# Second block of a two-block layer: attention output in its own tiles, no sums on GpSimd, a denser interleave of the state space branch

## The chip, the cores and the metric

The kernel runs on one core of one Trainium2 chip. The metric is the device time of one execution in microseconds (us); lower is better. The five engines are written as the profile writes them: PE (TensorE, with PEld for its weight loads), DVE (VectorE), ACT (ScalarE), POOL (GpSimd) and SP (SyncE, which here issues the DMAs).

## The reference, cut to what matters

A sequence of 1024 tokens of width 1024 passes two blocks. The first (attention, a gated delta rule, sixteen experts) is not touched. The second is, in outline:

```python
h = rms(x, norm1_g);  proj = h @ w_in
u, q, k, v, qi, ki, wi, gates = split(proj)
y_ssm = s5_branch(u, ...)              # complex state space scan, 32 groups of 64 states, gelu, GLU
# sparse attention, 8 blocks of 128 queries, 8 heads of 64, one shared key/value head
iscore = sum_h relu(qi_h . ki) * wi_h   # index scores, causal
idx = top_k(iscore, 256)                # 256 keys kept per query
y_att = softmax(q k[idx]^T / 8) v[idx]
g_ssm, g_att = split(gates)
merged = sigmoid(g_ssm) * (y_ssm @ w_proj_ssm) + sigmoid(g_att) * (y_att @ w_proj_attn)
x = x + merged @ w_out
x = x + (silu(h2 @ w_ffn_gate) * (h2 @ w_ffn_up)) @ w_ffn_down      # h2 = rms(x, norm2_g)
```

## The kernel before, in words

Products in float32 precision are made of three matmuls: each operand is split into a high and a low part (`split`: ACT rounds, a subtraction gives the rest), and `mm3` adds high*high, high*low and low*high in PSUM. Weights come the same way: `wunit` loads a raw tile, ACT makes `wh`, and `K.sub` (L76) makes `wl`. `K.sub` is VectorE's subtraction, except in the middle of `stage_attn`, where it is set to GpSimd's.

`stage_norm2` normalises the input in eight tiles of 128 tokens and leaves it transposed in `K.hh` and `K.hl`; in every second tile the product with the final gain (L1645) is GpSimd's. `idx_tile` and `q_tile` make index scores, keys, values and queries. `select` finds the 256 largest scores of each query by a search over 32 bits, two blocks at a time: one block's counts are ACT's (L1775), the other's DVE's (L1778), and a few one-column operations on DVE (L1781 to L1793) lead from one bit to the next. `attend` then computes one block of 128 queries in four steps (a generator, one `yield` a step): scores in the PSUM tile `lg`, a masked maximum on DVE (L1875), the exponential on ACT (L1878), a scaling (POOL for blocks 0 to 5, DVE for 6 and 7), transposes into `tp`, products with the values into `po`.

The state space branch (`s5`) is eight units of four groups. A unit loads five tables (`s5wi`, `s5u`, `s5cs`, `s5m`, `s5wo`), multiplies into a half of an `lg` tile (L57), and then runs a chain of eight steps, six on DVE and two on GpSimd (`s5a`, L1569, and `s5c`, L1573). One unit is issued per step of the last two attention blocks. `s5wo` has one buffer, the other tables two.

`gate_tile` computes 16 tiles of gates (48 matmuls each, PSUM tile `pj`, tanh on ACT, L1928). `attn_branch(c)` multiplies half c of the attention output by its projection: it reads the output back from DRAM (`uo<-yatd`), splits it into rows 4 to 7 of `K.hh` and `K.hl`, which the gates still read until all gate tiles of that half are done, and uses `pj` for half 0, `lg` and `tp` for half 1. `glu` and `merge` finish the two branches; in `merge` GpSimd adds the two (L2019).

The order on each engine is not the written one. A scheduler with its own model of durations places the instructions when the program is built, earlier code first where both could go; on the chip each engine then takes its instructions in that fixed order. So gate tiles, which depend on little, stand between the steps of `select` and `attend`, and how many are left for later follows from the written order.

Of the kernel before, what the change touches and what calls it, by code (L numbers as in the profile page):

```python
# [1538 lines left out]
def s5_states(K, wk, i, e):  # L1539


    nc = K.nc
    V, P = nc.vector, nc.gpsimd
    lo, hi = slice(0, 64), slice(64, 128)
    T = [128, 4, 128]
    g0 = 4 * i
    gs = slice(g0, g0 + 4)
    wi, wo, u = (wk.tile(T, F32, name="s5" + n, bufs=b) for n, b in (("wi", 2), ("wo", 1), ("u", 2)))
    m = wk.tile([128, 4, 240], F32, name="s5m", bufs=2)
    cs = wk.tile([128, 4, 256], F32, name="s5cs", bufs=2)  # L1550
    nc.sync.dma_start(wi, K.s5i[:, gs])
    nc.sync.dma_start(u, K.uTd[:, :, gs].rearrange("t p g c -> (t p) g c"))
    p0 = K.s5p[:, gs]
    nc.sync.dma_start(cs, bass.AP(tensor=p0.tensor, offset=p0.offset, ap=[[0, 2], [32 * 256, 64], [1, 1024]]))

    k0 = K.s5k[0:16, gs]
    nc.sync.dma_start(m.rearrange("p g x -> p (g x)")[:, 0:848],
                      bass.AP(tensor=k0.tensor, offset=k0.offset, ap=[[16, 8], [32 * 240, 16], [1, 848]]))
    nc.sync.dma_start(wo, K.s5o[:, gs])
    co, si = cs[:, :, 0:128], cs[:, :, 128:256]  # L1560
    e = e.rearrange("p (g c) -> p g c", g=4)
    for g in range(4):
        K.mm(e[:, g], wi[:, g], u[:, g], g == 0, True)

    a, r, z, c = (wk.tile(T, F32, name="s5" + n) for n in "arzc")
    V.tensor_mul(a, e, co)
    V.tensor_mul(r[lo], e[hi], si[hi])
    V.scalar_tensor_tensor(r[hi], e[lo], -1.0, si[lo], op0=ALU.mult, op1=ALU.mult)
    P.tensor_add(a, a, r)  # L1569
    for g in range(4):  # L1570
        V.tensor_tensor_scan(z[:, g], K.rho[:, g0 + g:g0 + g + 1].to_broadcast([128, 128]), a[:, g], 0.0,
                             op0=ALU.mult, op1=ALU.add)
    P.tensor_mul(c, z, co)  # L1573
    V.scalar_tensor_tensor(r[lo], z[hi], -1.0, si[hi], op0=ALU.mult, op1=ALU.mult)
# [51 lines left out]
def stage_norm2(K, hp, ps):  # L1626

    nc, I = K.nc, K.I
    K.hh = hp.tile([128, 8, L], F32R, name="hh")
    K.hl = hp.tile([128, 8, L], F32R, name="hl")  # L1630
    K.rs1 = K.cst.tile([128, 8], F32, name="rs1")
    with ExitStack() as s:
        wk = K.pool(s, "n2w", 2, side="right")
        fg = wk.tile([128, D], F32, name="fg", bufs=1)
        gg = wk.tile([128, D], F32, name="gg", bufs=1)
        nc.sync.dma_start(fg, I["final_g"].rearrange("(a n) -> a n", a=1).to_broadcast([128, D]))
        nc.sync.dma_start(gg, I["norm1_g_2"].to_broadcast([128, D]))
        nc.gpsimd.tensor_mul(gg, gg, fg)
        for t in range(8):
            ts = slice(t * 128, (t + 1) * 128)  # L1640
            x = wk.tile([128, D], F32, name="x", bufs=4)
            nc.sync.dma_start(x, K.xacc[ts])
            ss = wk.tile([128, 4], F32, name="ss")
            xf = wk.tile([128, D], F32, name="xf", bufs=3)
            (nc.gpsimd if t % 2 else nc.vector).tensor_mul(xf, x, fg)  # L1645
            jk = wk.tile([128, D], BF, name="jk", bufs=1)
            nc.scalar.activation(jk, x, AF.Square, accum_out=ss[:, 0:1])
            nc.scalar.activation(jk, xf, AF.Square, accum_out=ss[:, 1:2])
            r1 = K.rs1[:, t:t + 1]
# [207 lines left out]
def attend(K, wk, ps, b):  # L1857
# [3 lines left out]
    qt = wk.tile([128, 4, 128], F32, name="aqt")  # L1861
    nc.sync.dma_start(qt, K.qsd[b])
    qs = wk.tile([128, 2, 4, 128], F32R, name="aq", bufs=1)
    stack(K, qs, qt, nc.gpsimd.tensor_sub)
    for hp in range(2):
        po = ps.tile([128, 2, 2, 128], F32, name="po", bufs=1)
        for pp in range(2):
# [52 lines left out]
def gate_tile(K, wk, ps, f):  # L1920

    nc = K.nc
    w = hcols(K, 1476 + f * 128, 128)
    o = wk.tile([128, L], F32, name="uo")
    for c in range(2):
        cs = slice(c * 512, (c + 1) * 512)
        q = proj_T(K, ps, w, 0, 128, c * 512, 512)
        nc.scalar.activation(o[:, cs], q, AF.Tanh, scale=0.5)  # L1928
    nc.sync.dma_start(K.sgt[f], o)

# [5 lines left out]
    yield q[:, 512:1024]  # L1936


def attn_branch(K, wk, gk, tag, ps, c):

    nc = K.nc
    cs = slice(c * 512, (c + 1) * 512)
    h, l = K.hh[:, 4:8, cs], K.hl[:, 4:8, cs]
    for k0 in (0, 2):
        r = wk.tile([128, 2, 512], F32, name=tag)
        nc.sync.dma_start(r, K.yatd[:, k0:k0 + 2, cs])
        K.split(h[:, k0:k0 + 2], l[:, k0:k0 + 2], r)
    for f0 in (4, 6, 0, 2) if c else range(0, 8, 2):
        if c == 0 or f0 < 4:
            K.wpa[f0] = K.wblock(K.I["w_proj_attn_2"][0], f0 * 128, 256)  # L1950
        hs, ls = K.wpa[f0]
        g = gk.tile([128, 2, 512], F32, name=tag if c == 0 else "g", bufs=2 + 2 * c)
        nc.sync.dma_start(g, K.sgt[8 + f0:10 + f0, :, cs].rearrange("f p n -> p f n"))
        for i, q in enumerate((pair if c else narrow)(ps)):
            m = slice(i * 128, (i + 1) * 128)
            for k in range(4):
                K.mm3(q, (hs[k][:, m], ls[k][:, m]), (h[:, k], l[:, k]), k == 0, k == 3)
# [44 lines left out]
def merge(K, wk, ps, y):  # L2002
# [3 lines left out]
    for f0 in range(0, 8, 2):  # L2006
        hs, ls = K.wblock(K.I["w_proj_ssm_2"][0], f0 * 128, 256)
        for f in range(f0, f0 + 2):
# [5 lines left out]
            for c, q in enumerate(pair(ps)):  # L2014
# [1 line left out]
                for k in range(4):  # L2016
                    K.mm3(q, (hs[k][:, m], ls[k][:, m]), (y[:, 0, k, cs], y[:, 1, k, cs]), k == 0, k == 3)
                nc.vector.scalar_tensor_tensor(g[:, cs], g[:, cs], 1.0, q, op0=ALU.add, op1=ALU.mult)  # L2018
                (nc.gpsimd if f < 7 else nc.vector).tensor_add(g[:, cs], g[:, cs], a[:, cs])  # L2019
                nc.scalar.activation(A[:, f, cs], g[:, cs], AF.Copy, scale=0.5)  # L2020
                nc.vector.scalar_tensor_tensor(B[:, f, cs], g[:, cs], 0.5, A[:, f, cs].bitcast(F32), op0=ALU.mult,
                                               op1=ALU.subtract)
# [2 lines left out]
def stage_attn(K, hp, ew, dr):  # L2025
# [8 lines left out]
    with ExitStack() as s:  # L2034
# [9 lines left out]
        with ExitStack() as s1:  # L2044
# [40 lines left out]
        with ExitStack() as sw:  # L2085
# [3 lines left out]
                    pass  # L2089
            units = s5(K, sp, ps)  # L2090
            for _ in chain(attend(K, wk, ps, 6), attend(K, wk, ps, 7)):
                next(units)
            next(units)
        for f in list(range(8, 16)) + list(range(8)):
            gate_tile(K, fk, ps, f)
        K.wpa = {}
        attn_branch(K, fk, fk, "uo", ps, 0)
        sa.close()
        sr.close()
        bk = K.pool(s, "brw", 2)  # L2100
# [1 line left out]
        with ExitStack() as sy:  # L2102
            yp = K.pool(sy, "yap", 1, side="right")
            ya = yp.tile([128, 2, 4, L], F32R, name="ya")
            with ExitStack() as sg:
                gk = K.pool(sg, "glw", 2)
                attn_branch(K, bk, bk, "ma", ps, 1)
                glu(K, bk, gk, ps, ya)
            merge(K, bk, ps, ya)
        K.wh = w5  # L2110
        K.w5 = out2_units(K, range(4))
    K.pjb = None
    K.sub = nc.vector.tensor_sub
# [405 lines left out]
```

## Time and profile before

| | |
|---|---|
| median of three runs | 3204.37 us (3204.27 to 3206.47) |
| profiled execution, its own time | 3200.96 us |
| span in that profile | 3199.2 us |
| PE busy | 2898.8 us, 91% |
| DVE busy | 2396.0 us, 75% |
| ACT busy | 1634.3 us, 51% |
| POOL busy | 661.9 us, 21% |
| mean granted clock of PE, as a share of full speed | 0.953 |

Busy times are shares of the whole span, and the span is a row of stages with different limits. The second block's first half, which the change touches, runs from about 1767 to 2453 us. A time in a row is counted from the start of the span.

### The profile page before, as it was taken

The page shows a single profiled execution, that of the slowest core. Times are in us where ns is not written, and L with a number is a line of the kernel's source. Part 1 is how long each engine was busy: PE and PEld are TensorE (multiplying, and loading weights), DVE is VectorE, ACT ScalarE, POOL GpSimd, SP SyncE. Part 2 cuts the span into 40 slices and gives each one's busy share as a digit, 9 for nine tenths or more (in the row PEclk, how much of TensorE's full clock was granted, in tenths as well). Part 3 has the DMA queues.
Part 4 walks back from the last instruction along what each step waited for, and adds up shares of the span by engine and source line. Part 5 has one row for each costly group of instructions (what it writes and reads, how often), then busy time and mean ns, then how long its engine had stood idle before and what let it go on. Part 6 is the DMA issues. An engine that isn't in the chain of part 4 may idle for free.

```text
span 3199.2 us, 45340 instructions
## 1 busy us (share of the span) xinstructions
PE 2898.8 (91%) x15797; PEld 2389.5 (75%) x15797; DVE 2396.0 (75%) x4935; ACT 1634.3 (51%) x3127; POOL 661.9 (21%) x606
## 2 busy tenths in 40 slices
PE   6899998779898969999998799998798999999999
PEld 3677886768786748888776677777677788888787
DVE  4388676897887599999988599986556686555675
ACT  3333454464675238877776577654443243333343
POOL 1000111244555511112001334432125000000000
PEclk8999998789899979999999899999899999999999
DMA  6366565443325469999996223224565323333833
GB/s 219 109 212 194 178 189 185 128 140 111 89 89 181 146 227 379 393 393 375 374 372 222 69 66 93 69 71 129 156 220 192 111 77 107 110 109 99 293 112 102
DMA packets 366211, 567.04 MB, mean 177 GB/s; under 512 B 72581, under 2 KB 207646, under 8 KB 365982
## 3 DMA queue, kind: packets, MB, share of 16 engines
q1 hardware_dynamic: 361374, 547.37, 50.5%
q0 software_dynamic: 4608, 16.78, 2.1%
q8 instruction: 124, 2.03, 0.3%
q14 instruction: 105, 0.86, 0.1%
HBM read 446.12 MB, written 117.95 MB: 176 GB/s over the span
## 4 chain that ended last, share of the span: by engine, by line
PE 65%; DVE 18%; DMA 7%; issue 4%; ACT 3%; POOL 2%; SPq 1%; DVEq 0%; ACTq 0%; POOLq 0%
PE pj L57 38%; PE py L57 5%; PE pu L57 5%; PE pg L57 5%; PE ga L57 2%; PE lg L57 2%; DVE dst L707 2%; DMA s5wo<-s5o 1%; DVE E L723 1%; DVE bjv L1778 1%; DMA wmod<-in_w_mod_dram 1%; PE sc L57 1%; PE tp L1252 1%; PE gm L57 1%; DVE tw L1101 1%
## 5 line engine op out<-in xcount | busy, mean ns | idle before, releaser
L1229 DVE TENSOR_TENSOR wl<-wraw,wh 128x1024 fp32r<-128x1024 f32 x384 | 446.6, 1219 | 10.7 <-ACT wh L1228 10.4
L1228 ACT ACTIVATE wh<-wraw 128x1024 fp32r<-128x1024 f32 x384 | 391.8, 1060 | 77.7 <-PE pu L57 39.7
L57 PE MATMUL pj<-hh,wh 128*128 128x512 f32 (+1 forms) x768 | 297.7, 388 | 14.4 <-ACT uo L1928 9.5
L57 PE MATMUL pj<-hl,wh 128*128 128x512 f32 (+1 forms) x768 | 293.3, 382 | 0.0
L57 PE MATMUL pj<-hh,wl 128*128 128x512 f32 (+1 forms) x768 | 292.4, 382 | 0.0
L57 PEld LDWEIGHTS pj<-hh,wh 128*128 128x128 f32 x768 | 146.1, 190 | 46.5 <-ACT uo L1928 12.6
L57 PE MATMUL pj<-wh,hh 128*128 128x512 f32 (+1 forms) x400 | 160.8, 403 | 16.9 <-DVE g L2018 9.0
L57 PEld LDWEIGHTS pj<-hh,wl 128*128 128x128 f32 x768 | 145.4, 190 | 30.4 <-issue 3.7
L57 PEld LDWEIGHTS pj<-hl,wh 128*128 128x128 f32 x768 | 145.8, 190 | 27.1 <-issue 2.9
L708 ACT ACTIVATE E<-sc,dst 128x512 f32<-128x512 f32 (+1 forms) x192 | 117.4, 616 | 94.4 <-DVE dst L707 84.1
L57 PE MATMUL pj<-wh,hl 128*128 128x512 f32 (+1 forms) x400 | 158.9, 399 | 1.7 <-DVE hl L214 1.5
L57 PE MATMUL pj<-wl,hh 128*128 128x512 f32 (+1 forms) x400 | 160.2, 401 | 0.0
L75 ACT ACTIVATE wh<-wraw 128x1024 fp32r<-128x1024 f32 (+2 forms) x88 | 88.7, 1014 | 91.9 <-DMA wraw<-in_w_in_dram 37.3
L76 POOL TENSOR_TENSOR wl<-wraw,wh 128x1024 fp32r<-128x1024 f32 (+1 forms) x44 | 100.7, 2293 | 140.2 <-ACT wh L75 139.9
L57 PE MATMUL sc<-da_ka,da_qh 128*128 128x512 f32 (+1 forms) x192 | 83.6, 438 | 35.7 <-ACT E L708 32.0
L1292 POOL DMA_INDIRECT xacc<-ye,ix x16 | 49.9, 3121 | 318.7 <-DVE ye L1291 238.0
L707 DVE TENSOR_REDUCE dst<-sc 128x1 f32<-128x512 f32 (+1 forms) x192 | 108.6, 593 | 8.2 <-PE sc L57 7.2
L57 PE MATMUL pu<-wl,xh 128*128 128x512 f32 x256 | 101.3, 396 | 9.4 <-DVE wl L1229 9.2
L722 POOL TENSOR_TENSOR E<-E,dst 128x512 f32<-128x512 f32 (+1 forms) x96 | 95.7, 1024 | 55.8 <-DVE dst L719 27.2
L1775 ACT ACTIVATE bja<-isc,bca 128x384 bf16<-128x384 f32 (+2 forms) x96 | 79.4, 827 | 51.3 <-DVE bca L1793 25.4
L57 PEld LDWEIGHTS pj<-wh,hh 128*128 128x128 f32 x400 | 77.7, 195 | 34.8 <-DVE g L2018 9.4
L57 PE MATMUL pg<-wl,xh 128*128 128x512 f32 x256 | 102.8, 402 | 0.5 <-DVE wl L1229 0.5
(825 smaller groups left out, 8508.8 us busy)
## 6 DMA issues: line engine op xcount, KB each, us to landing
wraw<-in_w_gate_dram SPq DMA_DIRECT2D x64, 1024.0 KB
wraw<-in_w_up_dram SPq DMA_DIRECT2D x64, 1024.0 KB
wraw<-in_w_down_dram SPq DMA_DIRECT2D x64, 1024.0 KB
wraw<-in_w_in_dram SPq DMA_DIRECT2D x52, 512.0 KB
raw<-hsd SPq DMA_DIRECT2D x38, 512.0 KB
mw<-in_w_mod_dram SPq DMA_DIRECT2D x32, 512.0 KB
raw<-in_w_ffn_gate_dram SPq DMA_DIRECT2D x22, 512.0 KB
raw<-in_w_ffn_up_dram SPq DMA_DIRECT2D x22, 512.0 KB
```

Source lines behind the costliest of these rows:

```text
L57: self.nc.tensor.matmul(out, lhsT, rhs, start=start, stop=stop, skip_group_check=True)
L75: nc.scalar.activation(h, raw, AF.Copy)
L76: self.sub(l, raw, h.bitcast(F32))
L707: nc.vector.tensor_reduce(mn[:, i, j:j + 1], p[:, :n], axis=AX.X, op=ALU.min)
L708: nc.scalar.activation(e[:, c0:c0 + n], p[:, :n], AF.Exp, bias=mn[:, i, j:j + 1], scale=-1.0, accum_out=ls[:, i, j:j + 1])
L722: nc.gpsimd.tensor_mul(e1, e1, sc[:, 1, j:j + 1].to_broadcast([128, n]))
L723: nc.vector.scalar_tensor_tensor(e0, e0, sc[:, 0, j:j + 1], e1, op0=ALU.mult, op1=ALU.add)
L1101: self.V.tensor_tensor(b[:, :, i], a[:, :, 0], a[:, :, 1], op=ops[i])
L1228: nc.scalar.activation(h, raw[:, k], AF.Copy)
L1229: nc.vector.tensor_sub(l, raw[:, k], h.bitcast(F32))
L1292: nc.gpsimd.indirect_dma_start(out=K.xacc, out_offset=bass.IndirectOffsetOnAxis(ap=idx[e][:, :1], axis=0), in_=ye, in_offset=None, compute ...
L1775: self.K.nc.scalar.activation(jk[:, :self.n], self.x, AF.Sign, bias=cand, scale=-1.0, accum_out=cnt)
```

## The change

Six edits, all in the second block's first half.

1. `K.sub` stays VectorE's everywhere, so the low parts of the weights in `stage_attn` move from POOL to DVE. So do the gain product of every second tile in `stage_norm2`, the subtraction for the stacked queries in `attend`, both GpSimd steps of an s5 unit, and the sums in `merge`. The scaling of blocks 0 to 5 (L1882) stays on POOL.
2. `s5wo` gets a second buffer; the tile `s5c` takes the buffer of `s5a`.
3. Two s5 units are issued per step of the last two blocks, so that all eight are issued within the first five steps.
4. `attn_branch(0)` splits the attention output into two tiles of its own (`abh`, `abl`), and this (`attn_parts`) is written ahead of the gate tiles.
5. `attn_branch(0)` accumulates in `lg` and `tp` instead of `pj`.
6. `gate_tile` takes its PSUM tile directly; its matmuls are the same.

```diff
-    wi, wo, u = (wk.tile(T, F32, name="s5" + n, bufs=b) for n, b in (("wi", 2), ("wo", 1), ("u", 2)))
+    wi, wo, u = (wk.tile(T, F32, name="s5" + n, bufs=b) for n, b in (("wi", 2), ("wo", 2), ("u", 2)))
...
-    P.tensor_add(a, a, r)
+    V.tensor_add(a, a, r)
...
-    P.tensor_mul(c, z, co)
+    c = wk.tile(T, F32, name="s5c", tag="s5a")
+    V.tensor_mul(c, z, co)
...
-            (nc.gpsimd if t % 2 else nc.vector).tensor_mul(xf, x, fg)
+            nc.vector.tensor_mul(xf, x, fg)
...
-    stack(K, qs, qt, nc.gpsimd.tensor_sub)
+    stack(K, qs, qt, nc.vector.tensor_sub)
...
+def attn_parts(K, wk, tag, c, h, l):
+    for k0 in (0, 2):
+        r = wk.tile([128, 2, 512], F32, name=tag)
+        K.nc.sync.dma_start(r, K.yatd[:, k0:k0 + 2, c * 512:(c + 1) * 512])
+        K.split(h[:, k0:k0 + 2], l[:, k0:k0 + 2], r)
...
-        for i, q in enumerate((pair if c else narrow)(ps)):
+        for i, q in enumerate(pair(ps)):
...
-                (nc.gpsimd if f < 7 else nc.vector).tensor_add(g[:, cs], g[:, cs], a[:, cs])
+                nc.vector.tensor_add(g[:, cs], g[:, cs], a[:, cs])
...
-        K.sub = nc.gpsimd.tensor_sub
...
             for _ in chain(attend(K, wk, ps, 6), attend(K, wk, ps, 7)):
-                next(units)
-            next(units)
+                next(units, None)
+                next(units, None)
+        ap = K.pool(sr, "abr", 2, side="right")
+        h, l = (ap.tile([128, 4, 512], F32R, name="ab" + n, bufs=1) for n in "hl")
+        attn_parts(K, ap, "abi", 0, h, l)
         for f in list(range(8, 16)) + list(range(8)):
             gate_tile(K, fk, ps, f)
         K.wpa = {}
-        attn_branch(K, fk, fk, "uo", ps, 0)
+        attn_branch(K, fk, "uo", ps, 0, h, l)
```

What this does to the order, at three places. First DVE, late in the search over blocks 6 and 7, with block 5's attention between its bits (`bca`, `bcv` are the candidates, `bjv` a count, `as` the masked scores). Before:

```order
L1793 SCALAR_TENSOR_TENSOR bca<-bca,bma 128x1
L1904 TENSOR_TENSOR ay<-po,aol 64x256 x2
L1793 SCALAR_TENSOR_TENSOR bcv<-bcv,bmv 128x1
L66 TENSOR_TENSOR apl<-tp,aph 128x512
L1778 TENSOR_SCALAR bjv,bnv<-isc,bcv 128x1024
L66 TENSOR_TENSOR apl<-tp,aph 128x512
L1781 TENSOR_SCALAR bma<-bna 128x1
L1875 ISA as,ast<-lg,madd 128x768
L1875 ISA ast 128x1
L1875 ISA as,ast<-lg,madd 128x768
L1875 ISA ast 128x1
L1783 TENSOR_SCALAR bmv<-bnv 128x1
```

The same stretch of DVE now:

```order
L1779 TENSOR_SCALAR bjv,bnv<-isc,bcv 128x1024
L1782 TENSOR_SCALAR bma<-bna 128x1
L1784 TENSOR_SCALAR bmv<-bnv 128x1
L1794 SCALAR_TENSOR_TENSOR bca<-bca,bma 128x1
L1794 SCALAR_TENSOR_TENSOR bcv<-bcv,bmv 128x1
L1779 TENSOR_SCALAR bjv,bnv<-isc,bcv 128x1024
L1876 ISA as,ast<-lg,madd 128x768
L1876 ISA ast 128x1
L76 TENSOR_TENSOR wl<-wraw,wh 128x1024
L1876 ISA as,ast<-lg,madd 128x768
L1876 ISA ast 128x1
L1784 TENSOR_SCALAR bmv<-bnv 128x1
```

A gate tile's `wl` (L76), which was on POOL's list, now stands on DVE's between a search step and the next.

Second, ACT in the last attention block (`uo<-pj` is the tanh of a gate tile, L1928 before and L1930 now; `s5y` the output of an s5 unit; `as` the exponential). Before:

```order
L75 ACTIVATE wh<-wraw 128x1024
L1928 ACTIVATE uo<-pj 128x512
L65 ACTIVATE aph<-tp 128x512 x2
L1928 ACTIVATE uo<-pj 128x512
L65 ACTIVATE aph<-tp 128x512 x2
L1593 ACT_TABLE_LOAD
L1593 ACTIVATE s5y<-lg 128x512
L1878 ACT_TABLE_LOAD
L1878 ACTIVATE as,ast<-as,ast 128x1024
L65 ACTIVATE hh<-uo 128x2x512
L1901 ACTIVATE aol<-po 64x512
L75 ACTIVATE wh<-wraw 128x1024
```

ACT in that block now:

```order
L65 ACTIVATE aph<-tp 128x512 x4
L1594 ACT_TABLE_LOAD
L1594 ACTIVATE s5y<-lg 128x512
L1879 ACT_TABLE_LOAD
L1879 ACTIVATE as,ast<-as,ast 128x1024 x2
L1594 ACT_TABLE_LOAD
L1594 ACTIVATE s5y<-lg 128x512
L1879 ACT_TABLE_LOAD
L1879 ACTIVATE as,ast<-as,ast 128x1024
L65 ACTIVATE aph<-tp 128x512 x2
L1879 ACTIVATE as,ast<-as,ast 128x1024
L65 ACTIVATE aph<-tp 128x512 x2
```

The last two s5 outputs are reached in this block's first half, no gate tile is left in it, and the split of the attention output (`hh<-uo` before, `abh<-abi` now) comes two steps later.

Third, the end of `merge`. Before, POOL alternated between the low parts of weights and the sums:

```order
L76 TENSOR_TENSOR wl<-wraw,wh 128x1024
L2019 TENSOR_TENSOR g<-g,ma 128x512 x3
L76 TENSOR_TENSOR wl<-wraw,wh 128x1024
L2019 TENSOR_TENSOR g<-g,ma 128x512
L76 TENSOR_TENSOR wl<-wraw,wh 128x1024
L2019 TENSOR_TENSOR g<-g,ma 128x512 x2
```

DVE at the end of `merge` now (`hl` is the low part of the merged output):

```order
L2026 SCALAR_TENSOR_TENSOR hl<-g,hh 128x512
L2023 SCALAR_TENSOR_TENSOR g<-g,tp 128x512
L2024 TENSOR_TENSOR g<-g,ma 128x512
L2026 SCALAR_TENSOR_TENSOR hl<-g,hh 128x512
L2024 TENSOR_TENSOR g<-g,ma 128x512
L2023 SCALAR_TENSOR_TENSOR g<-g,lg 128x512
L2026 SCALAR_TENSOR_TENSOR hl<-g,hh 128x512
L2024 TENSOR_TENSOR g<-g,ma 128x512
L2026 SCALAR_TENSOR_TENSOR hl<-g,hh 128x512
L2023 SCALAR_TENSOR_TENSOR g<-g,tp 128x512
L76 TENSOR_TENSOR wl<-wraw,wh 128x1024
L2024 TENSOR_TENSOR g<-g,ma 128x512
```

Products, sums and low parts follow each other on one engine; POOL has none of them.

## Rows read from the trace of the kernel before

**Rows 1.** Busy time in four stretches: us, each engine (xinstructions), clock, DMA share, GB/s.

```profile
1780.00:1812.00 32.00, 28.23 (x152) 24.67 (x151) 23.43 (x54) 19.77 (x45) 14.22 (x20) 0.93 0.11 34
...
1860.00:2120.00 260.00, 240.69 (x1207) 199.40 (x1208) 250.05 (x873) 179.12 (x386) 100.26 (x82) 0.99 0.22 67
...
2178.00:2354.00 176.00, 140.10 (x779) 120.42 (x778) 109.25 (x199) 73.24 (x104) 43.53 (x33) 0.91 0.57 165
...
2406.00:2453.00 47.00, 38.02 (x167) 31.02 (x166) 36.06 (x34) 16.91 (x23) 36.53 (x20) 0.94 0.59 202
```

**Rows 2.** Chain of waits in `stage_norm2`: start us, us, what.

```profile
1801.15 2.94 POOL xf L1645
...
1807.27 1.20 DVE xf L1654
```

**Rows 3.** POOL's groups in the search, 1840 to 2164: xcount | busy, mean ns.

```profile
L1882 POOL TENSOR_TENSOR as<-as,ast 128x128 f32<-128x128 f32 (+5 forms) x48 | 45.9, 971 | 95.5 <-DVE bmv L1783 34.7 <-DVE ast L1880 20.7 <-DVE bca L1793 15.5
L76 POOL TENSOR_TENSOR wl<-wraw,wh 128x1024 fp32r<-128x1024 f32 x17 | 41.7, 2452 | 50.2 <-ACT wh L75 50.0
L1674 POOL TENSOR_TENSOR aq<-aqt,aq 64x512 fp32r<-64x512 f32 x14 | 18.3, 1304 | 13.9 <-ACT aq L1673 7.8 <-issue 4.6 <-POOL as L1882 0.8
```

**Rows 4.** Three of DVE's groups in the same stretch.

```profile
L1793 DVE SCALAR_TENSOR_TENSOR bcv<-bcv,bmv 128x1 uint32<-128x1 uint32 x90 | 25.5, 283 | 0.4
...
L1793 DVE SCALAR_TENSOR_TENSOR bca<-bca,bma 128x1 uint32<-128x1 uint32 x90 | 24.2, 269 | 0.3
...
L1781 DVE TENSOR_SCALAR bma<-bna 128x1 uint32<-128x1 f32 x95 | 14.1, 148 | 10.8 <-ACT bja L1775 10.0
```

**Rows 5.** Prices on DVE: groups of the whole first half, then of 2178 to 2354.

```profile
L76 DVE TENSOR_TENSOR wl<-wraw,wh 128x1024 fp32r<-128x1024 f32 x7 | 8.5, 1224 | 4.2 <-ACT wh L75 4.2
...
L66 DVE TENSOR_TENSOR apl<-tp,aph 128x512 fp32r<-128x512 f32 x25 | 16.8, 686 | 6.2 <-ACT aph L65 5.9
L1571 DVE TENSOR_TENSOR_SCAN s5z<-rho,s5a 128x128 f32<-128x128 f32 x32 | 10.9, 405 | 2.1 <-POOL s5a L1569 2.0
...
L1875 DVE CUSTOM_DVE_ANT_0 as<-lg,madd 128x1024 f32<-128x1024 f32 x8 | 9.7, 1218 | 1.1 <-PE lg L57 1.1
...
L1884 DVE TENSOR_SCALAR as<-as,ast 128x1024 f32<-128x1024 f32 x8 | 6.0, 749 | 0.2
L1567 DVE TENSOR_TENSOR s5r<-lg,s5cs 64x512 f32<-64x512 f32 x8 | 5.5, 693 | 0.1
```

**Rows 6.** SP's queue early in the branch: start us, us, what it issues.

```profile
2171.19 7.96 SPq L1557 DMA_DIRECT2D s5m<-s5k  x1
...
2183.63 10.25 SPq L1551 DMA_DIRECT2D s5wi<-s5i  x1
```

**Rows 7.** Size of one `s5cs` load, and a stretch in which one runs.

```profile
s5cs<-s5p SPq DMA_DIRECT2D x8, 512.0 KB
...
2173.00:2177.00 4.00, 4.00 (x30) 3.69 (x28) 0.00 (x0) 0.52 (x2) 0.00 (x0) 1.00 0.13 52
```

**Rows 8.** First step of the s5 units on DVE: all eight, then the second.

```profile
L1566 DVE TENSOR_TENSOR s5a<-lg,s5cs x8: 680/684/692, 2178.5 to 2339.6; 128x512 f32<-128x512 f32 x8
...
2196.36 0.68 DVE L1566 TENSOR_TENSOR s5a<-lg,s5cs 128x512 f32<-128x512 f32 x1
```

**Rows 9.** ACT's split of the attention output, with the idle time before it.

```profile
2297.00 1.06 ACT L65 ACTIVATE hh<-uo 128x1024 fp32r<-128x1024 f32 x1 [18.44 <-DMA uo<-yatd]
```

**Rows 10.** Chain of waits, 24 matmuls of one gate half in a row.

```profile
2128.03 5.46 PE pj L57 x24
```

**Rows 11.** End of `merge`: PE's wait, DVE's low parts, two pieces of the chain.

```profile
PE pj L57 <- DVE g L2018: 9.0, 1, 9.0
...
L2021 DVE SCALAR_TENSOR_TENSOR hl<-g,hh 128x512 fp32r<-128x512 f32 x15 | 25.0, 1674 | 8.6 <-ACT hh L2020 8.3
...
2444.15 3.94 DMA ma<-mad
...
2452.35 17.83 PE pj L57 x66
```

More of the change, by code (lines that the diff above doesn't have):

```diff
@@ L1563, in s5_states @@
         K.mm(e[:, g], wi[:, g], u[:, g], g == 0, True)
-    a, r, z, c = (wk.tile(T, F32, name="s5" + n) for n in "arzc")
+    a, r, z = (wk.tile(T, F32, name="s5" + n) for n in "arz")
     V.tensor_mul(a, e, co)
@@ L1924, in gate_tile @@
     o = wk.tile([128, L], F32, name="uo")
-    for c in range(2):
+    for c, q in enumerate(narrow(ps)):
         cs = slice(c * 512, (c + 1) * 512)
-        q = proj_T(K, ps, w, 0, 128, c * 512, 512)
+        for k in range(8):
+            K.mm3(q, (w[0][k], w[1][k]), (K.hh[:, k, cs], K.hl[:, k, cs]), k == 0, k == 7)
         nc.scalar.activation(o[:, cs], q, AF.Tanh, scale=0.5)
@@ L1936, in wide, with attn_branch @@
     yield q[:, 512:1024]
-def attn_branch(K, wk, gk, tag, ps, c):
+def attn_parts(K, wk, tag, c, h, l):
[3 more added lines that the diff above has]
+        K.split(h[:, k0:k0 + 2], l[:, k0:k0 + 2], r)
+def attn_branch(K, gk, tag, ps, c, h, l):
     nc = K.nc
     cs = slice(c * 512, (c + 1) * 512)
[L1943 to L1947, printed above, removed]
     for f0 in (4, 6, 0, 2) if c else range(0, 8, 2):
@@ L2106, in stage_attn @@
                 gk = K.pool(sg, "glw", 2)
-                attn_branch(K, bk, bk, "ma", ps, 1)
+                h, l = K.hh[:, 4:8, 512:1024], K.hl[:, 4:8, 512:1024]
+                attn_parts(K, bk, "ma", 1, h, l)
+                attn_branch(K, bk, "ma", ps, 1, h, l)
                 glu(K, bk, gk, ps, ya)
@@ L2112, in stage_attn @@
     K.pjb = None
-    K.sub = nc.vector.tensor_sub
 def out2_units(K, us):
```

## Prediction

> **What bounds the kernel now.** I read the table of engines first, then windows, one for each stage that the change touches, then groups by line, and last the chain of waits and single instructions. Over the whole span PE is 91% busy, so a cost elsewhere counts only where PE waits, and the stages differ in that. In the search (1860 to 2120) DVE is busy 250.05 of 260 us and PE 240.69: both are nearly full, DVE more so [rows 1]. In the last attention stretch (2178 to 2354) neither is: PE 140.10 of 176, DVE 109.25, at a granted clock of 0.91 and a DMA share of 0.57, so waits end it [rows 1]. At the end of `merge` (2406 to 2453) PE, DVE and POOL are within 2 us of one another [rows 1]. In 1780 to 1812, `stage_norm2`, PE lacks 3.8 us.
>
> **A. The gain product of `stage_norm2`.** The chain of waits runs through POOL's 2.94 us product, where DVE's takes 1.20 [rows 2]. PE idles 3.8 us of that window and runs at 0.93 [rows 1]; at full clock its 28.23 busy us would have been about 2 shorter. So 6 is the most that can go, and I take about two thirds: -4 (-7 to 0). Four more products of 1.2 on DVE are covered there, busy 23.43 of 32.
>
> **B. The search and the attention between its steps.** DVE takes over 17 `wl` and 14 subtractions for the stacked queries [rows 3]. It does the same `wl` in 1.224 us, and a product of 64x512 in 0.693 [rows 5]: 17 x 1.224 + 14 x 0.693 = 30.5 us more on an engine with 10 to spare in 260. Against it stands what GpSimd costs DVE. The step L1793 is one column wide, as L1781 is, yet takes 283 and 269 ns, not 148 [rows 4]. It has two tensor inputs, and I read the excess, 90 x 0.135 + 90 x 0.121 = 23 us, as time in which it waits for GpSimd. Of POOL's 105.9 us in this stretch 60.0 leave (41.7 + 18.3) and L1882's 45.9 stay [rows 3]; 60.0/105.9 of 23 is 13. The net is 17.5 us of DVE work. DVE idles 10.8 us ahead of L1781, 10.0 of it for ACT's count [rows 4]; there some of the new work fits without delay, but the order puts a `wl` also where nothing waits. I take half as path: +9 (0 if all 23 come back and the idle takes the rest; +17 if nothing fits in the idle; +30 if GpSimd's absence gives nothing back).
>
> The Trainium skill has a rule here, in "Perfetto Trace Analysis", section "Optimizing Scalar/DVE Operations": a saturated DVE may hand work to ScalarE or even GpSimd, though the latter shares a read port with it, so that this might not help. The first half speaks against the change, which loads the fullest engine; by it alone the sum would hold +30 here. The second half is what L1793's 283 against 148 ns looks like; by it alone the term would be near zero.
>
> **C. The state space branch and the last attention.** Two units per step would bring the eight units ahead of the old pace; what can hold them is their loads. A 512 KB `s5cs` load, when alone, keeps a DMA share of 0.13, two of sixteen engines, and moves 52 GB/s [rows 7], so one takes 524 KB / 52 GB/s = 10.1 us. The other four loads of the unit and the weights of gate tiles share these engines; SP stood blocked for 7.96 and 10.25 us in front of two of them [rows 6]. The first two units started 17.9 us apart (2178.5 and 2196.36), while nothing else of the program held the second [rows 8]. So I take 17 us per unit: the last starts at 2178.5 + 7 x 17 = 2297.5, not at 2339.6 [rows 8].
>
> The Trainium skill states the reason for two engines, in "DMA: Bandwidth & Descriptors", section "Rules for kernel authors": an outermost dimension of c < 16, such as a broadcast of c copies, confines a DMA to c engines. `s5cs` is loaded with two copies outermost, and the 0.13 agrees; by this rule the loads alone set the pace, and the two units per step bring nothing beyond it.
>
> What still stands on DVE behind the start of the last unit, by the order: the unit itself, 8 steps of about 0.69 and four scans of 0.405, 7.1 us; six rows of scores, each 1.218 + 0.749 + three one-column steps of 0.148, 14.5 us; 16 `apl` of 0.686, 11.0 us; two low parts of the attention output like a `wl`, 2.4 us [rows 4, 5]. That is 35; small ones and hand-overs from ACT and PE I put at 5, an estimate from 2 hand-overs per score row of which most lie beside other work. DVE is done at 2337.5. Then the order leaves 72 of the 96 matmuls of `attn_branch(0)`; 12 lie beside DVE's end, and 60 x 0.2275 us (5.46/24 [rows 10]) = 13.7 follow with nothing beside them. The half ends at 2351, against 2354 before: -3. With units 16 us apart and all hand-overs covered it is -12; with 19.5 it is +16. What goes is ACT's wait of 18.44 us for the attention output read back [rows 9], since the matmuls behind it no longer stand between gate tiles; what is late instead is the last attention block itself: its gate tiles are used up before, so PE idles beside DVE there, about 25 us, which before was filled.
>
> Moving the split ahead also moves two loads on SP ahead of gate weights. They need block 7's output for one half only (`c` = 0 reads the first four blocks, long written), so SP does not stop at them. The second `s5wo` buffer lets one load go earlier; that costs nothing. The two GpSimd steps per unit cost DVE 16 x 0.69 = 11 us in a stretch where it is 62% busy, and they save the hand-over to POOL, 2.0 us of waits in 32 scans [rows 5]: nothing either way, and counted in the 35.
>
> **D. The end of `merge`.** PE waited 9.0 us for `g` of L2018 [rows 11]. POOL alternates there between sums and `wl` and is busy 36.53 of 47 [rows 1], it gives `ma` buffers back late, and the chain then holds a 3.94 us load [rows 11]. DVE's low parts take 1674 ns each [rows 11], where an operation of that size alone takes 0.69 [rows 5]. With POOL empty I price DVE at 16 x (0.68 + 0.69 + 0.69) + 7 x 1.22 = 41.5 us [rows 5], and PE's 192 matmuls at 192 x 0.2275 = 43.7, so PE still ends last and the 9.0 goes. The 66 matmuls behind it took 0.27 each, not 0.2275 [rows 10, 11], 2.8 us more, which should go with the gap before them. What may be late next is DVE, 2.2 us below PE. I take -9 (-11 to -3).
>
> **Sum.** -4 + 9 - 3 - 9 = -7 us. On the profiled execution's 3200.96 (span 3199.2 and 1.8 around it) that is 3194. The median of the three runs is 3204.37, 3.4 above that execution, so I forecast 3197 for a median.
>
> **Rivals.**
>
> R1, slower: DVE becomes the bound and pays in full. The place is the search. The added 30.5 us return only by the 13 that I worked out and nothing fits in the idle (+17), because the idle lies between steps that depend on each other. Units then arrive at 18 to 19.5 us (+8 to +16 in C), with 25 us of idle PE that lowers the clock from its 2.4 GHz level on some stretches, as the 0.91 shows [rows 1]. With A and D at -4 and -9 the middle is +17 + 12 - 13 = +16, so 3220. For it: DVE is 96% busy there. Against: L1793's excess. It decides where `wl` costs DVE more than about 13 us above what comes back.
>
> R2, a larger gain: GpSimd's operations cost DVE more than L1793 shows, since any two-input step beside POOL is held up, as `hl` with its 1674 ns is [rows 11]. Then the search costs nothing, C ends 10 us earlier, and A and D give -13: -23, so 3181. For it: `hl`. Against: L1882, with 48 steps, stays in the search.
>
> R3, the change does not remove the two waits, it renames them. In D the sums join a chain of product, sum and low part on DVE; with some 6 us of hand-overs from PE and ACT on top of the 41.5, DVE ends 4 behind PE's 43.7, and of the 9.0 + 2.8 about 3 are left to gain, as the low end of D says. In A the product is not what PE waits for, and the term is 0. Then 0 + 9 - 3 - 3 = +3, so 3207. For it: PE lacks only 3.8 us in A; DVE and PE are 2.2 us apart in D. Against: the chain of waits names both.
>
> **How the numbers follow.** Forecast 0.45 (own range 3186 to 3206), R1 0.25, R2 0.17, R3 0.13. About 0.2%, 6.4 us, is what a measurement can tell from no change. Faster by that needs 3198 or less: a little over half of the forecast's case (0.25), all of R2, and a fifth of R3: 0.45. Slower needs 3211 or more: nearly all of R1 and a little of R3 and of the forecast: 0.27. Within: 0.28. The range runs from 3177 to 3217; it leaves out about the upper half of R1 and the lower third of R2.
>
> **What would show it.** In the changed profile: L1793 (now L1794) nearer 0.2 than 0.28 us per step, with DVE over 96% busy in the search (B right); an unchanged 0.27 means R1. The mask made after the last search step (`madd`) tells whether that stretch ends later. Eight starts of the first unit step 16 to 18 us apart (C right), 19 or more (R1). No `g` wait on PE at the end of `merge`, and `hl` near 0.69 (D right); a new one of some 6 us there, R3. No POOL step in the chain of `stage_norm2` (A right). I am wrong if the search ends more than 17 us later, or earlier at all, or if the time lies outside the range.

## The result, and the profile after

The changed kernel takes 3221.81 us (median of six runs, 3216.41 to 3226.16) against 3204.57: a ratio of 1.0056, 95% interval [1.0044, 1.0068]. It is slower by about 17 us; forecast were 3197, and a range to 3217. The profiled execution has a span of 3221.4 us, 22.2 above that of before.

The places of both profiles at which one stage ends and the next begins, as starts of single instructions in the two traces, show where the time went (one execution each, so a us or two in a row says little):

| start, us | before | after | the stage is longer by |
|---|---|---|---|
| first gain product of `stage_norm2` | 1767.0 | 1768.8 | |
| last transpose of `stage_norm2` (L1658, now L1659) | 1809.8 | 1811.2 | -0.4 |
| last `madd` of the search | 2164.0 | 2169.3 | +3.9 |
| first step of the first unit | 2178.5 | 2186.9 | |
| first step of the last unit | 2339.6 | 2324.9 | |
| last product of the attention (`po`) | 2337.5 | 2370.1 | |
| first matmul of `attn_branch(1)` | 2351.8 | 2383.9 | +26.8 |
| first matmul behind `merge` | 2452.35 | 2475.27 | -9.2 |

One stage made the loss: from the end of the search to `attn_branch(1)`. The first hardly moved, the second rose a little, the last fell; the block itself starts 1.8 us later. The windows of the changed kernel that answer to [rows 1], the last of them moved to where `attn_branch(1)` to `merge` now lie:

```profile
1780.00:1812.00 32.00, 28.40 (x151) 24.89 (x150) 25.99 (x59) 20.34 (x46) 11.31 (x16) 0.93 0.14 49
1860.00:2120.00 260.00, 243.13 (x1218) 201.22 (x1216) 251.88 (x893) 178.18 (x385) 57.92 (x56) 0.99 0.23 71
2178.00:2354.00 176.00, 122.20 (x618) 102.92 (x617) 104.54 (x197) 67.22 (x93) 0.74 (x7) 0.84 0.45 128
2384.00:2476.00 92.00, 88.23 (x388) 72.24 (x387) 68.83 (x93) 41.08 (x53) 0.00 (x0) 1.00 0.68 239
```

In 2178 to 2354 PE is busy 122.20 us where it was 140.10, DVE 104.54 where it was 109.25, and the granted clock is 0.84 instead of 0.91: no engine became the bound, all of them waited more. Next PE's waits from 2165 to 2480 (us in total, times, longest):

```profile
PE lg L57 <- DMA s5m<-s5k: 24.4, 3, 14.1
PE lg L57 <- DVE s5r L1568: 11.0, 2, 6.6
PE lg L57 <- DVE ast L1876: 6.0, 4, 2.6
...
PE pj L57 <- DVE g L2023: 2.0, 1, 2.0
```

The first row was not there before: PE, which takes its instructions in order, stands 24.4 us at matmuls of the units whose table `s5m` has not landed, with gate and attention matmuls queued behind. The longest of these waits, in PE's own order (start us, us, what, wait before it):

```profile
2221.76 2.05 PE L57 MATMUL lg<-s5u,s5m 128*128 128x128 f32 x8 [14.08 <-DMA s5m<-s5k]
```

The last row of the waits answers to the 9.0 us of [rows 11]. The chain of waits of the same stretch, its DMA pieces of over 10 us (start us, us, what):

```profile
2170.24 18.72 DMA s5m<-s5k
...
2202.94 18.68 DMA s5m<-s5k
...
2288.33 18.43 DMA sgt<-uo
...
2308.41 16.36 DMA s5cs<-s5p
```

72 of the stage's 215 us are four transfers of 424 to 512 KB that take 16 to 19 us each, where 10.1 for an `s5cs` alone was worked out from [rows 7]. The third is not even a table but the store of a gate: SP stands at the read back of `sgt` until it has landed, and the last units' loads stand behind.

The units (first step on DVE: starts of all eight, and what DVE waited for), against [rows 8]:

```profile
L1566 DVE TENSOR_TENSOR s5a<-lg,s5cs x8: 680/692/692, 2186.9 to 2324.9; 128x512 f32<-128x512 f32 x8
its engine sat idle before it (us, times) until:
  DMA s5cs<-s5p: 22.5, 3
  PE lg L57: 8.1, 4
```

138.0 us for seven intervals are 19.7 each (16.1, 35.7, 17.1, 16.7, 15.9, 16.6, 20.0), where the forecast had 17 and before 23.0 (17.9, 32.2, 17.9, 17.0, 36.6, 22.4, 17.1). The 35.7 holds PE's wait of 14.1 us for `s5m`; the other six are 17.05 each. And the split of the attention output, which the change writes ahead of the gates:

```profile
L1945 SPq DMA_DIRECT2D abi<-yatd x2: 376/408/441, 2343.9 to 2345.8; - x2
L65 ACT ACTIVATE abh<-abi x2: 1048/1052/1057, 2348.4 to 2350.7; 128x1024 fp32r<-128x1024 f32 x2
```

It is 51 us later than before, where ACT's `hh<-uo` stood at 2297.00 [rows 9].

Last, what terms B and D were to be judged by, DVE in the search and in `merge`. First the search, the window and two of its groups before:

```profile
1840.00:2164.00 324.00, 297.94 (x1487) 246.38 (x1485) 304.75 (x1012) 219.05 (x469) 119.62 (x95) 0.99 0.24 73
L76 DVE TENSOR_TENSOR wl<-wraw,wh 128x1024 fp32r<-128x1024 f32 x2 | 2.5, 1226 | 0.9 <-ACT wh L75 0.9
L1851 DVE TENSOR_TENSOR_SCAN sc<-onesr,se 128x384 f32<-128x384 bf16 (+5 forms) x6 | 13.7, 2290 | 0.0
```

The other group of before is that of [rows 4]. Now, with the end of `merge` in the last line:

```profile
1840.00:2169.30 329.30, 305.07 (x1509) 250.82 (x1508) 311.40 (x1049) 221.30 (x472) 64.61 (x64) 0.98 0.25 74
L76 DVE TENSOR_TENSOR wl<-wraw,wh 128x1024 fp32r<-128x1024 f32 x20 | 25.3, 1263 | 0.7 <-ACT wh L75 0.6
L1675 DVE TENSOR_TENSOR aq<-aqt,aq 64x512 fp32r<-64x512 f32 x14 | 9.6, 686 | 0.4
L1852 DVE TENSOR_TENSOR_SCAN sc<-onesr,se 128x384 f32<-128x384 bf16 (+5 forms) x6 | 9.7, 1614 | 0.0
L1794 DVE SCALAR_TENSOR_TENSOR bcv<-bcv,bmv 128x1 uint32<-128x1 uint32 x90 | 17.9, 199 | 0.4
L1794 DVE SCALAR_TENSOR_TENSOR bca<-bca,bma 128x1 uint32<-128x1 uint32 x90 | 17.8, 197 | 0.2
L1782 DVE TENSOR_SCALAR bma<-bna 128x1 uint32<-128x1 f32 x96 | 14.2, 148 | 6.2 <-ACT bja L1776 5.0
...
L2026 DVE SCALAR_TENSOR_TENSOR hl<-g,hh 128x512 fp32r<-128x512 f32 x16 | 10.8, 686 | 0.0
```

The one-column step fell from 283 and 269 to 199 and 197 ns [rows 4], which gives back 7.6 + 6.5 = 14 us, and the low parts in `merge` from 1674 to 686 ns [rows 11]. In the search 22.8 us of `wl` and 9.6 of subtractions came to DVE, 32.4 in all, and its busy time rose by 6.7: some 26 us came back, the 14 of that step, 4.0 of the scans, and the rest in small pieces of other steps.

### The profile page after: what moved, and what is told of

The parts are those of the page before. It is cut to its first block, busy times and chain, and to the rows that moved or that the text cites. A ratio compares the mean times of both kernels' runs of the same rounds, so it can differ in the third digit from the quotient of the medians.

```text
span 3221.4 us, 45307 instructions
## 1 busy us (share of the span) xinstructions
PE 2914.7 (90%) x15797; PEld 2401.2 (75%) x15797; DVE 2420.1 (75%) x5021; ACT 1638.9 (51%) x3130; POOL 501.3 (16%) x520
## 5 line engine op out<-in xcount | busy, mean ns | idle before, releaser
L57 PE MATMUL pj<-hh,wh 128*128 128x512 f32 (+1 forms) x736 | 284.4, 387 | 13.4 <-ACT uo L1930 10.1
L57 PE MATMUL pj<-hl,wh 128*128 128x512 f32 (+1 forms) x736 | 281.6, 383 | 0.0
L57 PE MATMUL pj<-hh,wl 128*128 128x512 f32 (+1 forms) x736 | 280.7, 383 | 0.0
L76 DVE TENSOR_TENSOR wl<-wraw,wh 128x1024 fp32r<-128x1024 f32 (+1 forms) x80 | 97.9, 1227 | 47.2 <-ACT wh L75 44.7
L57 PE MATMUL py<-wh,hl 128*128 128x512 f32 x256 | 98.7, 390 | 2.1 <-DVE hl L66 2.1
L57 PE MATMUL py<-wl,hh 128*128 128x512 f32 x256 | 100.0, 395 | 0.3 <-DVE wl L1229 0.3
```

Of the source, the lines that this page charges most:

```text
L57: self.nc.tensor.matmul(out, lhsT, rhs, start=start, stop=stop, skip_group_check=True)
L76: self.sub(l, raw, h.bitcast(F32))
```

## The experiments

Three readings of the lost stage were tried. T1: the table loads. T3: PE has nothing left beside the last attention block; later cut into T4 (`attn_branch(0)` is late since its own tiles lie where the unit tables lay), T5 (since `lg` and `tp` are held by others) and T6 (the denser order of units is late by itself). T2, the rival, blames DVE's added work. Each run is given by its ratio to the kernel before as measured beside it, and in us as ratio minus 1 times 3204.4; the interval of each is 3 to 6 us on either side. The changed kernel stands at +17.9.

**Fast tables.** The edit, in the changed kernel and in the kernel before; no engine's order but SP's differs by it:

```diff
-    nc.sync.dma_start(cs, bass.AP(tensor=p0.tensor, offset=p0.offset, ap=[[0, 2], [32 * 256, 64], [1, 1024]]))
+    for x in (0, 64): nc.sync.dma_start(cs[x:x + 64], p0)
```

In the changed kernel: 

> The changed kernel, with each s5cs load issued as two DMAs of 64 partitions each; on every engine but SP the order is the same. T1 (the transfers of the state space branch: s5cs goes through 2 of 16 engines, everything queued behind it on those two lands some 18 us later, and PE, DVE and SP wait in turn): the landings of 18.7, 18.7, 18.4 and 16.4 us in the chain of waits fall below 9 us, PE's wait of 14.1 us for s5m goes, the first unit step moves from 2186.9 to about 2179, the last from 2324.9 to below 2305, and the time falls from 3222 by 20 to 30 us, to 3192 to 3202. T2 (DVE carries GpSimd's work and is what is late): unchanged within 6 us, 3216 to 3228. T3 (PE has no gate tiles left beside the last attention block): the units come earlier but the stretch ends within 8 us of where it did, 3212 to 3222.

Measured: 3191.56 us, ratio 0.9958 [0.9945, 0.9972], -13.5 us against before, 31 faster than the changed kernel. T1 holds here in size and, in the main, in the trace: the landings shrink, though to 12 and 14 us and not below 9, and 4.7 us of PE's wait are left. PE's wait for `s5m`, and the long DMA pieces in the chain of the same stretch:

```profile
PE lg L57 <- DMA s5m<-s5k: 4.7, 1, 4.7
```

```profile
2171.53 12.31 DMA s5cs<-s5p
...
2183.86 14.19 DMA s5m<-s5k
...
2243.71 6.39 DMA sgt<-uo
2252.00 6.36 DMA uo<-sgt
```

A store of a gate takes 6.39 us, and the one that took 18.43 goes out at 2259.01 here, with the read back that stood behind it at 2265.24, though nothing of it was changed: I read this as a wait behind the tables on the same engines (no record names a packet's engine). The first unit starts at 2175.0, the last at 2293.5, 16.9 us apiece in the mean, and `attn_branch(1)` at 2351.7. Term C had 17, 2297.5 and 2351: with fast tables it comes out to within 4 us.

In the kernel before: 

> The kernel before, with each s5cs load issued as two DMAs of 64 partitions each; on every engine but SP the order is the same. T1: the same mechanism cost the kernel before less, since one unit per step leaves the transfers more time; its waits for s5wo (9.4 us) and part of the 18.4 us stall at the read back of the attention output go: 5 to 18 us faster than 3204.5, 3187 to 3200. T2 and T3 expect no more than 5 us.

Measured: 3175.00 us, 0.9904 [0.9889, 0.9919], -30.8 us, more than T1 had. Its two long intervals between units, 32.2 and 36.6, are 22.2 and 21.1 here. The slow load cost the kernel before as much as the changed one. So T1 is right about what a stage with these loads costs and wrong about the change: with fast tables the two kernels are still 17 us apart (3191.56 to 3175.00).

**Edit 1 alone, and its parts.** The edit takes GpSimd out of the two s5 steps (without the new buffers), the gain product, the query subtraction and the sums of `merge`, and drops both lines that set `K.sub`.

Edit 1: 

> The kernel before with edit 1 alone: no K.sub, gain product, query subtraction, unit step or merge sum on GpSimd. T1 (and the prediction's terms A, B and D without C): -4 + 9 - 9 = -4, so 3195 to 3207. T2 (the loss comes from DVE): 12 to 25 us slower than before, 3216 to 3230. T3 has no say, as T1.

Measured: 3191.01 us, 0.9964 [0.9953, 0.9976], -11.5 us, faster than T1 and T2 had. T2 falls: with all of that work on DVE and nothing else changed, the kernel is faster.

`merge` alone, with `K.sub` VectorE's from `attn_branch(1)` on:

```diff
-                (nc.gpsimd if f < 7 else nc.vector).tensor_add(g[:, cs], g[:, cs], a[:, cs])
+                nc.vector.tensor_add(g[:, cs], g[:, cs], a[:, cs])
...
+        K.sub = nc.vector.tensor_sub
         bk = K.pool(s, "brw", 2)
```

> The kernel before with the sums of merge on DVE, and K.sub on DVE from attn_branch(1) on; ahead of that its order is the same. The prediction's term D alone: -9 (-11 to -3), 3193 to 3201. If the wait of 9 us on PE is only renamed: within 3 us of before.

Measured: 3190.35 us, 0.9960 [0.9945, 0.9975], -12.8 us: all that edit 1 brings. PE's wait and DVE's low parts at the end of `merge`:

```profile
PE pj L57 <- DVE g L2018: 2.2, 1, 2.2
```

```profile
L2021 DVE SCALAR_TENSOR_TENSOR hl<-g,hh 128x512 fp32r<-128x512 f32 x16 | 10.8, 689 | 0.0
```

Edit 1 without the weights' low parts:

```diff
         K.wh = wh
+        K.sub = nc.gpsimd.tensor_sub
...
+        K.sub = nc.vector.tensor_sub
         bk = K.pool(s, "brw", 2)
```

> Edit 1 without its part on the low parts of the weights: K.sub is GpSimd's from the search to the last gate tile, as before, all else of edit 1 is DVE's. The prediction's term B: the weights' low parts cost DVE more than comes back, so this is 3 to 8 us faster than edit 1 alone, 3183 to 3188. If DVE gets all of it back: 3188 to 3196.

Measured: 3198.78 us, 0.9983 [0.9971, 0.9994], -5.4 us, 6 slower than edit 1 where the forecast's B had it 3 to 8 faster (the intervals overlap a little). L1793 stands at 310 and 264 ns there, 201 and 197 in edit 1 alone.

**Edits 3, 4 and 5.** One unit per step in the changed kernel:

```diff
-                next(units, None)
-                next(units, None)
+                next(units)
+            next(units)
```

> The changed kernel, with one unit per step of the last two attention blocks again (edit 3 undone, the other five kept). T1: the loads are asked for later and each has more time, so a good part of the loss goes: 3198 to 3212. T2: unchanged, 3216 to 3228. T3: some gate tiles stand beside the last attention again, so like T1, 3200 to 3212; the PE wait for s5m and the idle beside the last attention in its trace tell T1 from T3.

Measured: 3215.85 us, 1.0037 [1.0023, 1.0050], +11.9: 6 us off the changed kernel, with overlapping intervals, where T1 and T3 had at least 10. Edit 4 undone:

```diff
...
-        attn_parts(K, ap, "abi", 0, h, l)
         for f in list(range(8, 16)) + list(range(8)):
             gate_tile(K, fk, ps, f)
         K.wpa = {}
+        h, l = K.hh[:, 4:8, 0:512], K.hl[:, 4:8, 0:512]
+        attn_parts(K, fk, "uo", 0, h, l)
```

> The changed kernel with edit 4 undone (the split written behind the gate tiles, into rows of K.hh and K.hl; the accumulation in lg and tp kept). T4 (the own tiles lie in the space of the s5 tables, so their loads wait for the last unit and attn_branch(0) stands behind everything): the loads come earlier, the time falls by 12 to 28 us from 3222, to 3194 to 3210. T5 (lg and tp are held by the units and the transposes, so the scheduler finds no place for attn_branch(0) between them, whatever tiles it reads): PE's order keeps 252 of the matmuls that follow the attention in one piece, and the time stays within 6 us, 3216 to 3228.

Measured: 3234.44 us, 1.0089 [1.0074, 1.0104], +28.5: slower than the changed kernel, which neither theory had. The loads of the split did come earlier, at 2289.0 instead of 2343.9, as T4 said; the time did not follow. Edit 5 undone:

```diff
-        for i, q in enumerate(pair(ps)):
+        for i, q in enumerate((pair if c else narrow)(ps)):
```

> The changed kernel with edit 5 undone (accumulation in pj again; the own tiles and the early written split kept). T5: the time falls by 12 to 28 us, to 3194 to 3210. T4: the loads of abi stay behind the last unit, near 2340, and the time stays within 6 us, 3216 to 3228. If each holds a part (the order puts 48 of the matmuls between the last attention steps, behind the last unit), the time falls by some 8 us, to about 3214.

Measured: 3221.88 us, 1.0052 [1.0038, 1.0066], +16.7: no difference; T5 fails here. Both undone:

> The changed kernel with edits 4 and 5 undone (only edits 1, 2, 3 and 6 left; attn_branch(0) stands between the steps of the last attention block again). T4 and T5 together: the whole loss and more returns, 3184 to 3200, near the 3191 of edit 1 alone. T6 (two units per step, with the gates used up ahead, is the loss): still 3208 or more.

Measured: 3239.93 us, 1.0111 [1.0094, 1.0128], +35.6. T4 and T5 fail as the cause of the loss in this form, and T6 is left: edit 3 on top of edit 1 (with edit 2, of which below) costs 47 us, and 4 and 5 hide part of that.

To take the loads out of it, the same with the fast tables:

> Edits 1, 2, 3 and 6 (4 and 5 undone), with s5cs loaded by two DMAs of 64 partitions. With the slow load these edits stood 49 us above edit 1 alone (3240 to 3191). T1 (two units per step fail because the tables cannot be there in time): with the fast load nearly all of the 49 goes, to 3158 to 3178, near the 3163.6 of edit 1 with the fast load. T6 (the denser interleave is late by itself, since it puts unit steps ahead of attention steps on DVE and PE): 3185 to 3212, only the 28 us that every kernel gained so far.

Measured: 3197.91 us, 0.9978 [0.9966, 0.9989], -7.0: as T6 had it, and some 20 us above T1's range.

> The changed kernel with one unit per step, and with s5cs loaded by two DMAs of 64 partitions: edits 4 and 5 without edit 3, the tables early. T4 and T5 (attn_branch(0) stands behind the last attention block whatever the loads do): 3183 to 3195, some 22 to 30 us above the 3163.6 of edit 1 with the fast load. T1 alone (the loads are all of it): 3160 to 3175.

Measured: 3184.71 us, 0.9944 [0.9927, 0.9961], -17.9, as T4 and T5 had it. And edit 1 with the fast tables:

> The kernel before with edit 1 and with s5cs loaded by two DMAs of 64 partitions. If the two gains (11.6 and 27.7 us) are of different places, they add: 3163 (3158 to 3170). If the earlier tables only move the wait to DVE, which has edit 1's work: 3172 or more.

Measured: 3163.62 us, 0.9868 [0.9849, 0.9888], -42.3: the two gains add. It is the fastest kernel of this study, with `b_lead_cs16` below. So, in us against the kernel before (edit 2 stands in the last three rows):

| | tables slow | tables fast |
|---|---|---|
| edit 1 | -11.5 | -42.3 |
| 1 and 3 | +35.6 | -7.0 |
| 1, 4 and 5 | +11.9 | -17.9 |
| all, the change | +17.9 | -13.5 |

The column of fast tables lies 30 us below the other, and 43 where edit 3 stands without 4 and 5. Within each column edit 3 costs 47 or 35 alone, edits 4 and 5 cost 23 or 24, and all three 29. They do not add; that each takes away something that the other would have hidden is my reading.

What edit 3 does is read from the traces with the fast tables. With it the last unit starts at 2306.5 instead of 2316.8, 10 us earlier, and the last attention product at 2346.7 instead of 2311.6, 35 later. The order has 112 attention matmuls in a row behind the last unit, and 0 without the edit. The windows of the two, first with edit 3 and then without:

```profile
2280.00:2320.00 40.00, 34.27 (x186) 28.78 (x185) 31.55 (x59) 17.18 (x23) 0.21 (x2) 0.96 0.43 138
2320.00:2350.00 30.00, 19.91 (x110) 15.48 (x108) 18.71 (x38) 15.36 (x26) 0.25 (x1) 0.89 0.15 27
```

```profile
2280.00:2320.00 40.00, 37.84 (x225) 32.20 (x223) 34.34 (x62) 15.92 (x23) 0.44 (x3) 1.00 0.68 210
2320.00:2350.00 30.00, 26.88 (x120) 21.64 (x121) 18.49 (x27) 9.31 (x14) 0.00 (x0) 1.00 0.88 290
```

In 2320 to 2350 of the first, PE, DVE and ACT are all busy two thirds of the time or less, and at a clock of 0.89: the steps of one attention block hand over to one another with nothing beside them. The units would have to end 35 us earlier to pay for it, and they do not, because their pace hardly depends on the order in these two: (2306.5 - 2175.1)/7 = 18.8 us with two per step, (2316.8 - 2176.7)/7 = 20.0 with one.

Whether a smaller step that way costs anything:

```diff
             units = s5(K, sp, ps)
+            next(units)
             for _ in chain(attend(K, wk, ps, 6), attend(K, wk, ps, 7)):
                 next(units)
-            next(units)
```

> Edit 1 with the fast s5cs load, and the units begun one attention step earlier (still one per step, so the eighth is issued ahead of the last step). T6 (what edit 3 costs is the order: units ahead, attention steps behind them with little beside them, whatever the loads do): a small form of edit 3, 4 to 16 us above 3163.6, 3168 to 3180, and the last attention product comes later than the last unit's first step by more than before (2311.6 and 2316.8 in edit 1 with the fast load). If only the density counts, two units at once for one set of buffers: within 4 us, 3160 to 3168.

Measured: 3164.88 us, 0.9874 [0.9859, 0.9888], -40.4: no difference from -42.3. One step of lead (in the order, 32 attention matmuls in a row between the last unit's first and last products) costs nothing that can be measured, though T6 had 4 to 16 us and the last attention product does come later, 9.3 us behind the last unit's first step instead of 5.2 ahead of it. So T6 as an order that costs by itself missed here: edit 3's price is either that of a longer lead or that of two units at once, and no run tells these apart.

Edit 2 alone on top of edit 1:

> Edits 1, 2 and 6 (3, 4 and 5 undone). If edit 2 (the second s5wo buffer, s5c in the buffer of s5a) costs nothing, as the prediction had it: 3187 to 3196, as edit 1 alone (3191.0). If edit 2 has a part in the loss of each kernel that had it: 3200 or more.

Measured: 3196.03 us, 0.9975 [0.9966, 0.9984], -8.0, against -11.5 with overlapping intervals: at most a few us.

Edits 4 and 5 apart, with one unit per step and fast tables. Edit 5 only:

> The changed kernel with one unit per step, the fast s5cs load and edit 4 undone: of the two edits on attn_branch(0) only edit 5, the accumulation in lg and tp. T5 (lg and tp put it behind the attention): 3178 to 3190, as the 3184.7 with both. T4 (the own tiles do): 3160 to 3172.

Measured: 3171.87 us, 0.9903 [0.9887, 0.9919], -31.1. Edit 4 only:

> The changed kernel with one unit per step, the fast s5cs load and edit 5 undone: only edit 4, the own tiles. T4 (they lie in the space of the s5 tables, so the split waits for the last unit): 3178 to 3190, as the 3184.7 with both, with PE's wait of about 12 us for abh in its trace. T5: 3160 to 3172.

Measured: 3190.91 us, 0.9956 [0.9942, 0.9969], -14.1. So it is T4 in the main: of -42.3, edit 4 takes 28, edit 5 takes 11, both 24 (up to 4 of each may be edit 2). PE's wait for the split with edit 4 only; with edit 5 only, where the split goes to `hh`, PE has no wait for it:

```profile
PE pj L57 <- ACT abh L65: 12.6, 1, 12.6
```

PE's waits with edits 4 and 5, one unit per step and fast tables, and the loads of that kernel:

```profile
PE lg L57 <- ACT abh L65: 12.8, 1, 12.8
PE lg L57 <- issue: 9.3, 1, 9.3
```

```profile
L1945 SPq DMA_DIRECT2D abi<-yatd x2: 359/440/522, 2311.3 to 2312.5; - x2
L65 ACT ACTIVATE abh<-abi x2: 1040/1040/1041, 2318.1 to 2319.0; 128x1024 fp32r<-128x1024 f32 x2
```

The last attention product is at 2289.8 there, the last unit's first step at 2295.1, and the loads go out 16 us behind it. Written ahead of sixteen gate tiles, the split runs after the last unit. The trace shows when: SP issues the loads right behind the store of the last unit's output (`ysd<-s5y`). The code suggests why: the pool of its tiles is opened where the pool of the unit tables was closed, on the same side. No run puts the tiles elsewhere. All 96 matmuls of `attn_branch(0)` then follow in one piece, with nothing left for PE to do while it waits for them.

## Why the prediction was wrong

**A, the gain product: -4 forecast, -0.4 in the profile.** The last product takes 1.22 us now instead of 2.93, but the last transpose comes 42.4 us behind the first product, where it came 42.8, and PE in 1780 to 1812 is busy 28.40 us at 0.93, as before. The step "I take about two thirds" failed: the product left the chain of waits and the stage did not get shorter, as R3 had it for this term.

**B, the search: +9 forecast, +3.9 in the profile.** DVE's new work was sized rightly, 32.4 us against 30.5. What came back was not: 26 us, twice the 13 of the forecast. On L1793 it was 14, so the share taken there was good; but I had looked for GpSimd's price in that one step, and the scans and other steps paid it too. R2 was right in this. Half of the net as path was about right (3.9 of 6.7). By the times, too, little is left of B: edit 1 gains 11.5 us and `merge` alone 12.8. The Trainium skill ("Perfetto Trace Analysis", section "Optimizing Scalar/DVE Operations") says that work moved between GpSimd and DVE, which share a read port, might not help. The trace agrees, seen from the other side: DVE took over 32.4 us and its other steps became 26 us shorter. The +30 did not come.

**C, the state space branch and the last attention: -3 forecast, +26.8 in the profile.** This is the step that failed, in its first term: "I take 17 us per unit: the last starts at 2178.5 + 7 x 17 = 2297.5". It started at 2324.9, 27.4 later. Of these, 8.4 are the first unit, which I left in its place though the search ended 5.3 later, and 19.0 the pace of 19.7, nearly all of it (18.7) one interval of 35.7 in which PE stood 14.1 us at a table. What followed the last unit was priced nearly right: 45.2 us to the last attention product (40 forecast), then 13.8 (13.7 forecast). So 17 was right between stops, and the term had no stop in it. With fast tables the sum holds, 2293.5 and 2351.7 for 2297.5 and 2351: what it had wrong was what the slow loads do. I had read the pace from the first interval alone, 17.9; the next was 32.2 and a later one 36.6 in the kernel before, and fast tables cut these two to 22.2 and 21.1.

The choice of 17 had a rule beside it that should have weighed more. The Trainium skill says, in "DMA: Bandwidth & Descriptors", section "Rules for kernel authors", that an outermost dimension of a size c under 16 confines a transfer to at most c engines. The runs agree: the same bytes in two transfers of 64 partitions took some 30 us off both kernels. What I did not see is that other transfers are held up as well, a gate's store for 18.43 us, and SP with it.

I also priced edit 4 wrongly, at nothing: "SP does not stop at them", since their data are long written. The data were ready, and still the loads went out behind the last unit's store, 19 us after its first step. In the change itself the last attention hides most of this; with one unit per step and fast tables edit 4 costs 28 us.

Some sums of the term are off as well. The half ended at 2351.8 before, where the first matmul of `attn_branch(1)` stands, and not at 2354, the end of a window; so the same sum gives -1 and not -3. Seven intervals of 18 to 19.5 us give +4 to +14.5 by the forecast's sum, not the +8 to +16 of R1, and 16 with all 5 us of hand-overs covered give -15, not -12.

**D, the end of `merge`: -9 forecast, -9.2 in the profile**, and -12.8 [-17.6, -8.0] by the run that does it alone. The mechanism was right in each part: the wait fell from 9.0 to 2.0, the low parts from 1674 to 686 ns, and the 110 matmuls that follow in a row take 25.56 us where they took 28.02.

**The rivals.** R1's time, 3220, is what came out, but by luck: its search that pays in full (+17) was +3.9, and its units of 18 to 19.5 us are 19.7 only as a mean of one stop and six intervals of 17.05. R3 is refused in `merge` by D's 9.2 us and was right on A; R2 is refused by C and was right on the search. None of the rivals had what the runs show behind C: two losses, 35 to 47 us by edit 3 and 28 by the own tiles (24 together with edit 5), which cover one another in part.

Open is what holds the units at 17 to 20 us each once the tables come fast, and whether edit 3 costs by its lead or by two units at once.

## What to carry to other kernels

Work that is put ahead in the order is only ahead if it can run there; otherwise an engine that runs in order stands at it, and what filled its waits is used up before or comes alone behind. Read a pace from all intervals of a row of units, and find out what made the long ones, before taking the shortest as the rule. Before edits are judged together, run them apart: here one part gained 12.8 us, two lost, and with fast tables their separate losses of 35 and 24 were 29 together.

## What the hardware showed beyond that

The `s5cs` loads of 512 KB, with a DMA share of 0.13 in the stretch of [rows 7], slowed transfers that have no data in common with them: a gate's store of the same size took 18.43 us, and 6.39 us or less once the loads were reshaped. SP was held by them too: the longest issue of a single load, 9.12 us in the changed kernel between 2165 and 2360, was 4.72 with fast tables. A low part on DVE took 1674 ns while GpSimd ran sums and subtractions beside it, and 686 to 689 ns without, 2.4 times; six scans of the search fell from 2290 to 1614 ns each in the mean.
